# Two-layer hybrid decoder step: eight-step convolutions laid between matmul blocks, and S5 products held back by a count of recent instructions

## The chip, the cores and the metric

The kernel runs on one core of one Trainium2 chip. The metric is the device time of one execution in microseconds (us). The engines are named as the profile names them: PE (TensorE, with PEld for its weight loads), DVE (VectorE), ACT (ScalarE), POOL (GpSimd) and SP (SyncE, which here only issues DMAs).

## The reference

For 288 token columns (one prompt of 256 tokens and eight sequences of four new tokens) two layers are computed, each of a mixer, a feed-forward part and an embedding part. What the change touches is in the mixer:

```
z = x @ w_in                                   # 2048 -> u (1024), cv (1024), cg (1024)
y5, h = _s5(u, ...)                            # 64 groups: B u, complex scan over tokens, C h + D u
g5 = gelu(y5); s5_out = g5 * sigmoid(g5 @ s5_w_glu)
c = cv * sigmoid(cg)                           # GLU
c, new_conv = causal_dwconv(c, conv_buf, conv_w, conv_b)   # depthwise, 31 taps
c = silu(LN(c))
mix = concat(s5_out, c) @ w_out
```

The feed-forward part (2048 to 2 x 5632 and back, with a 3-tap convolution) and the embedding part follow, each with a LayerNorm. All is float32.

## The kernel before, in words

**Large products.** Weights come as blocks of 128 x 128, eight to a 512 KB load on SP (`stream_dma`, line 183). ACT makes a rounded half `whi`, DVE the rest `wlo`. `run` (line 354) works through a phase's list of blocks; each block is three matmuls of 288 columns into one accumulator (lines 379, 384, 385). At every second block `next_block` (line 217) calls `tick` (line 259), which emits what else is due.

**The planner.** The program is written out by a planner in Python, in a fixed order for every engine. It carries a clock `pe_t` for PE: 400 ns for a block, 500 for a convolution step, 400, 1000 and 1500 for the three kinds of S5 product. Deferred work (`defer`, `at`, generators that `wait`) is emitted when that clock, or a count of ticks, has come far enough.

**Phases of the mixer.** `u0` gives the first four u chunks. Then for j = 0..7 phase `p{j}` (32 blocks) gives the value and gate half of conv chunk j, and for j = 1..4 a phase `v{j}` (16 blocks) gives a further u chunk. Then comes `g` (64 blocks, the product with `s5_w_glu`, whose inputs are the S5 results), then `o`.

**A conv chunk.** When both halves of chunk j are there, ACT and DVE make the GLU into `cbuf` (one buffer, loaded with the cached rows by POOL at the start of loop j, line 1225), and POOL sends it to DRAM (`cb_d`, line 1246). `stack(j)` (line 1182) reads it back in four shifted copies (four DMAs on POOL, for j = 7 on SP) and sends the new cache rows out. `taps(j)` (line 1178) loads the tap weights `cw` (one buffer, 512 KB, POOL). `conv(j)` (line 1204) then makes the chunk in eight steps; each step is four matmuls of 32 weight columns and 256 token columns (line 1215) and four of 32 token columns (line 1218), each carried out in two passes, so 16 matmuls and 16 weight loads. Then ACT copies the result with the bias to `cvo`, and `ln_acc` takes it into the LayerNorm sums.

**Order around it.** At the end of phase `p{j}` the whole of `conv(j - 2)` stands, with a `tick` ahead of each step; then `taps(j - 1)`, the GLU if it was not yet emitted, and `stack(j)` (lines 1250 to 1256). `conv(6)` and `conv(7)` stand in the phase `g`: after 20 blocks of it `conv(6)` and `taps(7)`, after 12 more `conv(7)` (lines 1276 to 1281). While `conv(5)` is made, `split_g` splits S5 results for `g`, one per step from step 4 on. In the phase `g` itself, `xs_g` splits whatever is ready, at each block.

**S5.** The S5 runs as generators beside this, in eight chunks c. Each has small matmuls of 32 weight columns: `inject` (64 matmuls, line 1013), `project` (96, line 1042) and, in layer 0 and for layer 1 ahead of time, `s5_steps` (16, line 800), all through `strips` (line 395) or line 807. Between them stand a scan on DVE, elementwise work on ACT and POOL, and trips through DRAM on SP's and POOL's queues (`ust`, `tm`, `y_d`).

Of the kernel before, what the change touches and what calls it, by code (L numbers as in the profile page):

```python
# [16 lines left out]
SEQ = 256  # L17
# [47 lines left out]
L0_LAG = 4000.0  # L65
LOOK = 1
FREE_LAG = 500.0
EARLY_LAG = 7000.0
EARLY_RATE = 0.5
EV_GAP = 10  # L70
# [88 lines left out]
class Core:  # L159
    def __init__(self, tc, a, ctx):  # L160
        self.tc, self.nc, self.a, self.ctx = tc, tc.nc, a, ctx
        self.V = Meter(self, tc.nc.vector)
        self.pe_t = self.pe_l = self.dve_t = self.dve_c = 0.0
        self.freed = []
        self.scan = None
        self.rate = SETUP_RATE
        self.bg = []
        self.late, self.timed = [], []
        self.evq, self.ev_pos, self.acc_n = [], 0, 0
        self.lz, self.lz_n = None, 0  # L170
        self.pos = 0
        self.next_dma = 0
        self.next_hi = 0
        self.next_lo = 0
        self.raw = {}
        self.sub = {}
        self.nblk = DEPTH * NBLK
        self.early = {}


    def stream_dma(self, upto):
# [67 lines left out]
    def run_timed(self, force=False):  # L249
        for x in list(self.timed):  # L250
            if force or x[0] <= self.pe_t:
                self.timed.remove(x)
                x[1]()

    def flush(self):
        while self.late:
# [96 lines left out]
    def run(self, blocks, xs, evac, sums=None, wide=False):  # L353

        nc = self.nc
        tot, seen, accs = sums or self.sums(blocks)
        k0, pend = blocks[0][1], []
        for _, k, m in blocks:
            if pend and k != k0:
                for out, w, xl in pend:  # L360
                    nc.tensor.matmul(out, w, xl, start=False, stop=False)  # L361
                pend = []
            w = self.next_block()
            if m not in accs:
                if wide and len(accs) == 4:
                    accs[m] = (1 << 30, self.ps.tile([P, 512], F32, tag="one", name="acc5", bufs=1))
                else:
                    t = self.acc_tile()
                    accs[m] = (self.acc_n, t)
            out = accs[m][1][:, :TOK]  # L370
            n = seen[m]
            first, last = n == 0, n == tot[m] - 1
            if len(w) == 1:
                self.pe_t += 485.0
                nc.tensor.matmul(out, w[0], self.x32[k], start=first, stop=last)
            else:
                xh, xl = xs(k)
                self.pe_t += 400.0
                nc.tensor.matmul(out, w[0], xh, start=first, stop=False)  # L379
                if k == k0 and not last and (pend or not seen[m]):  # L380
                    nc.tensor.matmul(out, w[1], xh, start=False, stop=False)  # L381
                    pend.append((out, w[0], xl))
                else:
                    nc.tensor.matmul(out, w[0], xl, start=False, stop=False)  # L384
                    nc.tensor.matmul(out, w[1], xh, start=False, stop=last)  # L385
            seen[m] += 1
            if last:
                a, t = accs.pop(m)
                self.evq.append((a, lambda m=m, t=t: evac(m, t[:, :TOK])))
            if self.evq and self.pos - self.ev_pos >= EV_GAP:  # L390
                self.evict()
        while self.evq:
            self.evict()

# [405 lines left out]
    def s5_steps(self, bs, pw, kp):  # L800

        nc = self.nc
        kps = self.ps.tile([P, 512], F32, tag="one", name="kps", bufs=1)
        self.pe_t += 400.0
        for i in range(2):
            for q in range(4):
                nc.tensor.matmul(kps[32 * q:32 * q + 32, :4 * CIN], bs[:, q, i].rearrange("p g c -> p (g c)"),
                                 pw[:, q, i, 0:4].rearrange("p k o -> p (k o)"), start=(i == 0), stop=(i == 1),
                                 tile_position=(0, 32 * q))
        kv = kps[:, :4 * CIN].rearrange("p (k o) -> p k o", o=CIN)  # L810
        for g in range(2):
            nc.scalar.activation(kp[:, 3:7, g], kv, AF.Copy, scale=self.mask2[:, g:g + 1])
# [47 lines left out]
    def s5(self, l, mp):  # L860
# [88 lines left out]
        def make_o(c, cc, bc=None):  # L949

            if early:
                pk = cc
            else:
                yield from self.s5_out(l, c, cc, bc, pw, bs, work)
                yield from self.wait(PJ_LAG)
                while state["y"]:
                    yield None
                state["k"] = True
                self.s5_steps(bs, pw, kp)
                self.at(PS_LAG + 500.0, lambda: state.update(k=False))  # L960
                yield None
                k0 = kp[:, 3].rearrange("p g o -> p (g o)")
                V.scalar_tensor_tensor(k0, self.eye, self.prm("s5_d", c), k0, op0=OP.mult, op1=OP.add)
                kd = self.dp.tile([P, 7 * 2 * CIN], F32, tag="k_d", name="k_d", bufs=2)
                G.dma_start(kd, kp.rearrange("p k g o -> p (k g o)"))
                pk = pw[:, :, :, 1:5]
            while state["p"] < c - 1:
                yield None
            of = om.rearrange("p q i (r g o) -> p (q i) r g o", g=2, o=CIN)
            pf = pk.rearrange("p q i k o -> p (q i) k o")  # L970
            for g in range(2):
                h = slice(g * ST, (g + 1) * ST)
                nc.scalar.activation(of[h, :, :, g], pf[h], AF.Copy)
            if early:
                self.at(PS_LAG, lambda: state.update(o=c))
                return

            def back():
                load_t(c, kd)
                self.at(LOAD_LAG, lambda: state.update(o=c))  # L980
            self.at(BACK_LAG, back)
# [17 lines left out]
        def inject(us):  # L999
            v = self.ps.tile([P, 2, 512], F32, tag="two", name="bu", bufs=1)  # L1000
            self.pe_t += 1000.0
            for q in range(4):
                for i in range(2):
                    self.strips(v[:, i, q * NCH:(q + 1) * NCH], em[:, q, i], us[:, q], True, True)
# [37 lines left out]
        def project(c, us):  # L1042
            y = self.ps.tile([P, 512], F32, tag="one", name="y", bufs=1)
            self.pe_t += 1500.0
            for q in range(4):
                o = y[:, q * NCH:(q + 1) * NCH]
                self.strips(o, tms[c % 2][:, q], us[:, q], True, False)
# [56 lines left out]
        def main():  # L1104
# [3 lines left out]
            tb = tables(0)  # L1108
            initial()
            for c in range(S5C):  # L1110
                while c not in ready or state["e"] < c:
                    yield None
                self.rate = RATE[l]
                v = inject(us[c])
# [15 lines left out]
        def tail(c, us):  # L1130
            yield from self.wait(PJ_LAG)
            while finals:
                finals.pop(0)()
            while state["o"] < c or state["k"]:
                yield None
            state["y"] = True
            y = project(c, us)
# [21 lines left out]
    def mixer(self, l, ph):  # L1159
        nc, a = self.nc, self.a  # L1160
        V = self.V
        with self.tc.tile_pool(name="mx", bufs=1) as mp:
# [40 lines left out]
                    gsplit.add(c)  # L1203
                    n -= 1

            def conv(j):
                st, cw = stacks.pop(j), cws.pop(j)
                o = self.acc_tile()
                for k in range(8):
                    self.tick()  # L1210
                    self.pe_t += 500.0
                    if j == CVC - 3 and k >= 4:
                        split_g(n=1)
                    for b in range(4):
                        nc.tensor.matmul(o[32 * b:32 * b + 32, :SEQ], cw[:, b, k], st[:, b, 4 * k:4 * k + SEQ],  # L1215
                                         start=(k == 0), stop=False, tile_position=(0, 32 * b))
                    for b in range(4):
                        nc.tensor.matmul(o[32 * b:32 * b + 32, SEQ:TOK], cw[:, b, k], window(st, b, CW + 4 * k),
                                         start=False, stop=(k == 7), tile_position=(0, 32 * b))
                nc.scalar.activation(cvo[j], o[:, :TOK], AF.Identity, bias=self.prm("conv_b", j))  # L1220
                self.ln_acc(cst, cvo[j], j == CVC - 1)

            for j in range(CVC):
                cb = mp.tile([P, CBW], F32, tag="cbuf", name="cbuf", bufs=1)
# [2 lines left out]
                cbuf[j] = (cb, d)  # L1227
                part = {}

                def ev(m, acc):  # L1230
                    t = mp.tile([P, TOK], F32, tag="cvt", name="cvt", bufs=3)
                    if m < 16:
                        nc.scalar.activation(t, acc, AF.Copy, scale=0.5)
# [13 lines left out]
                        part["done"] = True  # L1247
                    self.defer(2, glu)
                self.run(ph[f"p{j}"], self.xs, ev)
                if j > 1:  # L1250
                    conv(j - 2)
                if j:
                    taps(j - 1)
                while "done" not in part:
                    self.late.pop(0)[1]()
                stack(j)
                if j in U_AT:
                    self.run(ph[f"v{j}"], self.xs, ev_u)

# [14 lines left out]
                self.split_x(m, w, 0.25)  # L1274
            sums = self.sums(ph["g"])
            self.run(ph["g"][:G_CUT[0] - 12], xs_g, ev_g, sums)
            conv(CVC - 2)
            taps(CVC - 1)
            self.run(ph["g"][G_CUT[0] - 12:G_CUT[0]], xs_g, ev_g, sums)
            self.finish(scan)  # L1280
            conv(CVC - 1)

            def fill(z):
                self.run(ph["g"][G_CUT[z]:G_CUT[z + 1]], xs_g, ev_g, sums)
# [347 lines left out]
```

## Time and profile before

| | |
|---|---|
| runs | 2738.88, 2741.99, 2744.91 us; median 2741.99 |
| the profiled execution's own time | 2743.43 us |
| its span, first to last instruction | 2741.6 us |
| mean granted clock | 0.991 |
| busy: PE / PEld / DVE / ACT / POOL | 97% / 95% / 66% / 49% / 11% |
| mixer of layer 0, about | 0 to 300 us |
| mixer of layer 1, about | 1378 to 1670 us |

The timeline's rows read: start, duration, engine, line, operation, output and inputs, sizes, count, and in brackets the idle time of the engine before it with what ended it ("issue": nothing that the profile shows). Matmuls overlap in the pipeline, so the pitch from start to start is their cost, not their duration. In a row of the windows, each engine's busy time stands with the number of its instructions, then the granted clock of PE (1.00 is full), the DMA engines' busy share and GB/s.

### The profile page before, as it was taken

Reading aid. Unit: us, or ns where it says so; the run is one execution under the profiler, and the core shown is the slowest. Engines: PE = TensorE matmul, PEld = TensorE weight load, DVE = VectorE, ACT = ScalarE, POOL = GpSimd, SP = SyncE. Lnnn points to the kernel's source line nnn. Section 1 sums busy time; section 2 is a strip of 40 time slices with the busy share of each in tenths; the row PEclk is TensorE's granted clock in tenths of the full one; section 3 lists DMA queues with packets and bytes.
Section 4 is the critical chain, followed back from the end, with each engine's and each line's share of the span. In section 5 each row is a group of like instructions: output and inputs, shape, how many; then the busy total and the mean of one; then the engine's idle time right before and its main releaser. Section 6 shows DMA issues by size and latency. Waiting matters only on the chain. (4 is left out here: it accounts for less than half of the span.)

```text
span 2741.6 us, 57943 instructions
## 1 busy us (share of the span) xinstructions
PE 2660.2 (97%) x23696; PEld 2600.8 (95%) x23696; DVE 1808.4 (66%) x3016; ACT 1352.9 (49%) x2224; POOL 305.0 (11%) x913
## 2 busy tenths in 40 slices
PE   8898999999999999999998899999999999999997
PEld 7887999999999999999987889999999999999997
DVE  6885768665677546667876558676546664566686
ACT  3453547553455345546464435565435553455363
POOL 3442001000011000000034410010000000000000
PEclk9999999999999999999999999999999999999998
DMA  7988444456566654554468775445554555455442
GB/s 236 254 249 248 151 153 162 162 192 190 186 190 197 201 167 159 174 172 153 164 191 257 229 204 180 154 159 171 175 169 157 169 174 171 156 169 176 164 151 102
DMA packets 188042, 496.12 MB, mean 181 GB/s; under 512 B 46369, under 2 KB 72241, under 8 KB 187521
## 3 DMA queue, kind: packets, MB, share of 16 engines
q1 hardware_dynamic: 174592, 444.00, 49.9%
q0 software_dynamic: 13184, 48.42, 6.2%
q8 instruction: 186, 3.05, 0.5%
q14 instruction: 80, 0.65, 0.1%
HBM read 472.11 MB, written 24.87 MB: 181 GB/s over the span
## 5 line engine op out<-in xcount | busy, mean ns | idle before, releaser
L379 PE MATMUL acc<-xh,whi 128*128 128x288 f32 x4656 | 1377.4, 296 | 8.1 <-ACT e L1333 3.2
L384 PE MATMUL acc<-xl,whi 128*128 128x288 f32 x4357 | 1288.0, 296 | 4.6 <-issue 3.7
L385 PE MATMUL acc<-xh,wlo 128*128 128x288 f32 x4357 | 1286.4, 295 | 0.0
L202 ACT ACTIVATE whi<-wraw 128x1024 fp32r<-128x1024 f32 x766 | 791.8, 1051 | 344.7 <-PE acc L384 206.1
L145 DVE TENSOR_TENSOR wlo<-wraw,whi 128x1024 fp32r<-128x1024 f32 x766 | 921.3, 1225 | 41.6 <-ACT whi L202 23.9
L379 PEld LDWEIGHTS acc<-xh,whi 128*128 128x128 f32 x4656 | 877.7, 189 | 15.8 <-ACT e L1333 4.1
L385 PEld LDWEIGHTS acc<-xh,wlo 128*128 128x128 f32 x4357 | 820.5, 188 | 3.9 <-issue 3.9
L384 PEld LDWEIGHTS acc<-xl,whi 128*128 128x128 f32 x4357 | 820.7, 188 | 3.0 <-DVE xl L145 2.5
L379 PE MATMUL acc<-hh,whi 128*128 128x288 f32 x1408 | 416.3, 296 | 0.0
L145 DVE SCALAR_TENSOR_TENSOR fo<-fe,parf,fo 128x304 f32<-128x304 f32 x352 | 188.2, 535 | 323.0 <-ACT fo L1366 316.6
L385 PE MATMUL acc<-hh,wlo 128*128 128x288 f32 x1312 | 387.7, 296 | 0.0
L384 PE MATMUL acc<-hl,whi 128*128 128x288 f32 x1312 | 386.9, 295 | 0.0
L379 PEld LDWEIGHTS acc<-hh,whi 128*128 128x128 f32 x1408 | 265.2, 188 | 0.5
L384 PEld LDWEIGHTS acc<-hl,whi 128*128 128x128 f32 x1312 | 247.0, 188 | 0.0
L385 PEld LDWEIGHTS acc<-hh,wlo 128*128 128x128 f32 x1312 | 246.6, 188 | 0.0
L1362 ACT ACTIVATE fe<-acc 128x256 f32<-128x256 f32 x176 | 67.4, 383 | 290.2 <-PE acc L385 290.2
L1372 POOL COPY fstage<-fe 128x9 f32<-128x9 f32 x176 | 44.5, 253 | 1038.1 <-ACT fe L1363 1016.7
L438 ACT ACTIVATE ln_q<-x 128x288 f32<-128x288 f32 x90 | 40.1, 446 | 221.1 <-DVE x L145 221.1
L1366 ACT ACTIVATE fo<-fe,parf 128x304 f32<-128x304 f32 x176 | 113.1, 642 | 16.7 <-ACT fe L1363 0.4
L145 DVE TENSOR_TENSOR x<-x,acc 128x288 f32<-128x288 f32 x64 | 29.1, 454 | 139.1 <-PE acc L385 139.0
L1386 ACT ACTIVATE hh<-fth 128x288 fp32r<-128x288 f32 x88 | 39.2, 445 | 163.5 <-DVE fth L145 163.5
L145 DVE SCALAR_TENSOR_TENSOR x<-x,acc 128x288 f32<-128x288 f32 x64 | 29.0, 453 | 122.9 <-PE acc L385 122.8
(251 smaller groups left out, 2340.7 us busy)
## 6 DMA issues: line engine op xcount, KB each, us to landing
wraw<-in_wts_dram SPq DMA_DIRECT2D x776, 512.0 KB
stack<-cb_d POOLq DMA_DIRECT2D x32, 282.0 KB, 9.3
cw<-in_convw_dram POOLq DMA_DIRECT2D x16, 512.0 KB, 5.3
big<-cb_d POOLq DMA_DIRECT2D x24, 282.0 KB, 9.6
cbuf<-in_convi_dram POOLq DMA_DIRECT2D x16, 283.5 KB, 9.6
cb_d<-cbuf POOLq DMA_DIRECT2D x16, 283.5 KB, 3.6
out_dram<-cb_d POOLq DMA_DIRECT2D x16, 283.5 KB, 11.5
sbt<-in_s5b_dram SPq DMA_DIRECT2D x15, 256.0 KB
```

Source lines behind the costliest of these rows:

```text
L145: return f(out, *args, **kw)
L202: self.nc.scalar.activation(hi, self.raw[s], AF.Copy)
L379: nc.tensor.matmul(out, w[0], xh, start=first, stop=False)
L384: nc.tensor.matmul(out, w[0], xl, start=False, stop=False)
L385: nc.tensor.matmul(out, w[1], xh, start=False, stop=last)
L438: nc.scalar.activation(st["q"], v, AF.Square)
L1362: nc.scalar.activation(e[:, 2:2 + SEQ], acc[:, :SEQ], AF.Copy)
L1366: nc.scalar.activation(o[:, :w], e[:, 2:EW], AF.Identity, bias=self.prm("ffn_conv_b", m), scale=self.prm("ffn_conv_w2", m))
L1372: nc.gpsimd.tensor_copy(stage[:, z, :, 0], e[:, SEQ:EW:6])
L1386: nc.scalar.activation(hh[i], h, AF.Copy, scale=0.5)
```

## The change

`conv(j)` no longer emits its steps; it gives back eight functions. For j = 0..5 they are put in `self.side`, and `run` emits one after each block of the phase that follows. `taps(j - 1)` and `stack(j)` are emitted after the last of them (`behind`), and the GLU of chunk j ahead of the first. `conv(6)` and `conv(7)` are emitted in one piece as before (`conv_now`, which first empties `side`). Besides, every small product notes a count of instructions with the planner's clock (32 for a conv step, 64, 128 and 192 for `s5_steps`, `inject` and `project`), and the three S5 products wait until those of the last 6000 ns and their own make at most 420.

```diff
+ISSUE_SPAN = 6000.0
+ISSUE_MAX = 420
...
+    def room(self, n):
+
+        self.issued = [x for x in self.issued if x[0] > self.pe_t - ISSUE_SPAN]
+        return sum(x[1] for x in self.issued) + n <= ISSUE_MAX
+
+    def spent(self, n):
+        self.issued.append((self.pe_t, n))
...
             if self.evq and self.pos - self.ev_pos >= EV_GAP:
                 self.evict()
+            if self.side:
+                self.side.pop(0)()
...
-                while state["y"]:
+                while state["y"] or not self.room(64):
...
-                while c not in ready or state["e"] < c:
+                while c not in ready or state["e"] < c or not self.room(128):
...
-            while state["o"] < c or state["k"]:
+            while state["o"] < c or state["k"] or not self.room(192):
...
-            def conv(j):
-                st, cw = stacks.pop(j), cws.pop(j)
-                o = self.acc_tile()
-                for k in range(8):
-                    self.tick()
+            def conv(j, behind=None):
+
+                st, cw, o = stacks.pop(j), cws.pop(j), []
+
+                def step(k):
+                    if not k:
+                        o.append(self.acc_tile())
                     self.pe_t += 500.0
+                    self.spent(32)
...
+                    if k == 7:
+                        nc.scalar.activation(cvo[j], o[0][:, :TOK], AF.Identity, bias=self.prm("conv_b", j))
+                        self.ln_acc(cst, cvo[j], j == CVC - 1)
+                        if behind:
+                            behind()
+                return [lambda k=k: step(k) for k in range(8)]
+
+            def conv_now(j):
+                while self.side:
+                    self.side.pop(0)()
+                for f in conv(j):
+                    self.tick()
+                    f()
...
                 self.run(ph[f"p{j}"], self.xs, ev)
-                if j > 1:
-                    conv(j - 2)
-                if j:
-                    taps(j - 1)
+
+                def behind(j=j):
+                    if j:
+                        taps(j - 1)
+                    stack(j)
                 while "done" not in part:
                     self.late.pop(0)[1]()
-                stack(j)
+                while self.side:
+                    self.side.pop(0)()
+                if j > 1:
+                    self.side = conv(j - 2, behind)
+                else:
+                    behind()
...
-            conv(CVC - 2)
+            conv_now(CVC - 2)
             taps(CVC - 1)
             self.run(ph["g"][G_CUT[0] - 12:G_CUT[0]], xs_g, ev_g, sums)
             self.finish(scan)
-            conv(CVC - 1)
+            conv_now(CVC - 1)
```

## Rows read from the trace of the kernel before

**Rows 1.** Windows: the two mixers and the stretch between (PE, PEld, DVE, ACT, POOL).

```profile
82.00:282.00 200.00, 180.21 (x3053) 160.41 (x3043) 143.56 (x252) 90.43 (x173) 72.92 (x136) 0.97 0.85 242
1392.00:1636.00 244.00, 223.09 (x3499) 205.69 (x3499) 145.05 (x213) 114.44 (x194) 85.29 (x154) 0.99 0.80 237
300.00:1360.00 1060.00, 1057.74 (x8069) 1053.57 (x8069) 719.48 (x1178) 540.53 (x881) 53.46 (x272) 1.00 0.53 175
```

**Rows 2.** Waits of PE (total us, times, longest us), five of the list.

```profile
PE y L399 <- issue: 4.3, 2, 2.8
PE acc L384 <- issue: 3.7, 1, 3.7
...
PE acc L1218 <- issue: 3.4, 3, 1.4
...
PE acc L379 <- issue: 2.2, 1, 2.2
...
PE acc L361 <- DVE xl L145: 1.5, 2, 1.0
```

**Rows 3.** Groups by line, PE: the conv matmuls of 256 columns, both buffers.

```profile
L1215 PE MATMUL acc<-big,cw 128*32 128x256 f32 x512 | 36.5, 401 | 5.8 <-issue 3.5 <-ACT xh L538 2.2
L1215 PE MATMUL acc<-stack,cw 128*32 128x256 f32 x512 | 33.9, 387 | 0.0
```

**Rows 4.** Timeline of PE, 107.9 to 113.3 us: one conv chunk and its neighbours.

```profile
108.28 0.29 PE L385 MATMUL acc<-xh,wlo 128*128 128x288 f32 x1
...
109.02 0.62 PE L1215 MATMUL acc<-stack,cw 128*32 128x256 f32 x8
...
111.99 0.62 PE L1215 MATMUL acc<-stack,cw 128*32 128x256 f32 x8
...
112.84 0.29 PE L381 MATMUL acc<-xh,wlo 128*128 128x288 f32 x1
112.97 0.29 PE L361 MATMUL acc<-xl,whi 128*128 128x288 f32 x1
```

**Rows 5.** Timeline of PE, 102.4 to 103.8 us: a lone product of 16 small matmuls.

```profile
102.71 0.29 PE L385 MATMUL acc<-xh,wlo 128*128 128x288 f32 x1
102.93 0.43 PE L807 MATMUL kps<-pw,bsm 128*32 128x64 f32 x16
...
103.53 0.29 PE L384 MATMUL acc<-xl,whi 128*128 128x288 f32 x1
```

**Rows 6.** The page, queues: the larger instruction queue (packets, MB, share).

```profile
q8 instruction: 186, 3.05, 0.5%
```

**Rows 7.** Windows, PE alone, from one "issue" wait's end to the next.

```profile
211.12:216.79 5.67, 4.16 (x126) 1.00 0.89 275
...
1461.66:1510.53 48.87, 44.97 (x886) 0.97 0.79 240
```

**Rows 8.** Timeline of PE: S5 products that waited in or just after a conv chunk.

```profile
151.32 0.33 PE L399 MATMUL y<-ust,tm 128*32 128x72 f32 x8 [1.55 <-ACT kp L812]
...
207.15 0.47 PE L399 MATMUL bu<-ust,em 128*32 128x72 f32 x17 [0.73 <-DMA ust<-u_d]
...
1504.70 0.41 PE L399 MATMUL bu<-ust,em 128*32 128x72 f32 x13 [1.14 <-ACT stb L996]
...
1539.71 0.47 PE L399 MATMUL bu<-ust,em 128*32 128x72 f32 x8 [3.57 <-DMA ust<-u_d]
```

**Rows 9.** The tile `cw`, 240 to 290 us: its two loads, issue to landing.

```profile
L1180 POOL DMA_DIRECT2D cw<-in_convw_dram x2: 538/548/557, 253.7 to 264.9; - x2
...
DMA to landing us min/median/max: 5.3/6.7/8.1
```

**Rows 10.** Timelines at the start of `g` in layer 0: PE, ACT, DVE.

```profile
246.60 0.29 PE L385 MATMUL acc<-xh,wlo 128*128 128x288 f32 x1
...
247.24 1.43 ACT L538 ACTIVATE xh<-u 128x288 fp32r<-128x288 f32 x4
...
252.31 0.53 DVE L145 SCALAR_TENSOR_TENSOR cbuf<-cvt 128x256 f32<-128x256 f32 x2 [9.11 <-DMA cbuf<-in_convi_dram]
```

More of the change, by code (lines that the diff above doesn't have):

```diff
@@ L178, in __init__ @@
         self.early = {}
+        self.side, self.issued = [], []
     def stream_dma(self, upto):
@@ L804, in s5_steps @@
         self.pe_t += 400.0
+        self.spent(64)
         for i in range(2):
@@ L1001, in inject @@
             self.pe_t += 1000.0
+            self.spent(128)
             for q in range(4):
@@ L1044, in project @@
             self.pe_t += 1500.0
+            self.spent(192)
             for q in range(4):
@@ L1214, in conv @@
                     for b in range(4):
-                        nc.tensor.matmul(o[32 * b:32 * b + 32, :SEQ], cw[:, b, k], st[:, b, 4 * k:4 * k + SEQ],
+                        nc.tensor.matmul(o[0][32 * b:32 * b + 32, :SEQ], cw[:, b, k], st[:, b, 4 * k:4 * k + SEQ],
                                          start=(k == 0), stop=False, tile_position=(0, 32 * b))
                     for b in range(4):
-                        nc.tensor.matmul(o[32 * b:32 * b + 32, SEQ:TOK], cw[:, b, k], window(st, b, CW + 4 * k),
+                        nc.tensor.matmul(o[0][32 * b:32 * b + 32, SEQ:TOK], cw[:, b, k],
+                                         window(st, b, CW + 4 * k),
                                          start=False, stop=(k == 7), tile_position=(0, 32 * b))
-                nc.scalar.activation(cvo[j], o[:, :TOK], AF.Identity, bias=self.prm("conv_b", j))
-                self.ln_acc(cst, cvo[j], j == CVC - 1)
+                    if k == 7:
[10 more added lines that the diff above has]
+                    f()
             for j in range(CVC):
@@ L1228, in mixer, with ev @@
                 part = {}
-                def ev(m, acc):
+                def ev(m, acc, cb=cb, d=d, part=part):
                     t = mp.tile([P, TOK], F32, tag="cvt", name="cvt", bufs=3)
```

## The prediction

> **What bounds the kernel now.** I read first the windows by stage. Between 300 and 1360 us PE is busy for 1057.7 of 1060 us: nothing that the change touches can help there. In the two mixers it is busy for 180.2 of 200 and 223.1 of 244 us, so 19.8 + 20.9 = 40.7 us are idle, while the DMA engines are at 0.85 and 0.80 against 0.53 elsewhere [rows 1]. So the mixer is bound by PE too, with waits worth 1.5% of the span strewn in.
>
> Then I read who ended those waits. "Issue" stands at 4.3 us (S5 products), 3.4 (inside conv chunks), 3.7 and 2.2 (plain blocks), seven waits and 13.6 us [rows 2]; the conv line shows another 3.5 [rows 3], but that one is the last chunk's and is `cw` landing late (below). The seven have a pattern. From the end of one to the next PE does 126 matmuls, or 886, which is 7 x 126.6 [rows 7]; with the weight loads 126 make 252 instructions, some 256 with the waits. The instruction queue moved 186 packets and 3.05 MB [rows 6], 16.4 KB each, 64 bytes for each of 256. So I take these waits for PE running out of instructions at the end of a packet. A packet lasts long in plain blocks (6 instructions in three pitches of 0.13 us, so 17 us) and 4.3 us in a conv chunk, whose 8 steps hold 256.
>
> The remaining idle time is S5 data arriving late and `cw`.
>
> **The change part by part.**
>
> *Laying the steps apart* adds PE time. In the chunk shown, the last block matmul starts at 108.28 and the second one behind the chunk at 112.84: 4.56 us, less two ordinary pitches of 0.13, leaves 4.30 for the chunk. Its middle steps come every (111.99 - 109.02) / 6 = 0.495 us [rows 4]. Eight make 3.96; the other 0.34 is what it costs to go from 128-column to 32-column matmuls and back, once. A lone product shows that this is paid by short groups as well: 16 small matmuls between blocks take 103.53 - 102.71 - 0.26 = 0.56 us [rows 5], with the same 0.22 us ahead of the first and 0.23 behind the first block matmul. A step alone between two blocks therefore costs 0.83 us, and eight of them 6.64 instead of 4.30. Chunks 0 to 5 are laid apart, in two layers: 12 x 7 x 0.336 = **+28.2 us**. The count of steps does not change (1024 matmuls of 256 columns, 16 chunks x 8 steps x 8 [rows 3]). This is all on PE, which is the bound, so I hide nothing of it here; what it covers is counted below.
>
> *"Issue" waits.* A laid step and its block are 38 instructions in 1.22 us, so a packet of them lasts 8.2 us instead of 4.3. That helps the 7.7 us that lie at products and in chunks. But a `project` is still 192 instructions in one piece, and with two steps behind it a packet is gone in under 4 us, less than the 5.67 us in which one packet was used up and still had to be waited for [rows 7]. The 3.7 and 2.2 us in plain blocks have no chunk near them. I take 70% of 7.7, **-5.4**; ends 0 and -13.6.
>
> *The count for S5 products* adds a wait in the planner. Laid steps come at 900 ns of its clock, at most seven in 6000 ns, 224; with `project` 416, under 420. So it holds something back only when two S5 products and several steps fall together. I price it at 0: a product moves by a few blocks, and what is queued behind it is its own chunk's scan. If it bit, S5 would reach `g` later; a late input there costs what the two shown cost, 1.5 together [rows 2].
>
> *S5 waits in or behind chunks.* Four, 1.55 + 0.73 + 1.14 + 3.57 = 7.0 us [rows 8]. They are waits for things set off at a given point of the planner's clock, and PE now takes longer per ns of it. Half, **-3.5**; ends 0 and -7.0.
>
> *DMAs that move with the step.* `taps(j - 1)`, the four loads of `stack(j)` and the store behind them now start after eight blocks of the next phase, 9.8 us (8 x 1.22) into it. On POOL they move behind the load of `cbuf(j + 1)` for j = 5 and 6. For chunks up to 5, 24 to 40 blocks remain, 9.5 us or more; the `cw` loads shown landed in 5.3 and 8.1 us [rows 9], so I take 0, and 2 at worst. On SP the loads of `stack(7)` wait for chunk 5 with weight units behind them; units are loaded three or four ahead, so 0. `cw` for `conv(6)` is another matter: before, 20 blocks lay between, now 12 (4.8 us). That is exactly the place of `conv(7)`, which waits 3.5 and 2.2 us for its `cw` today [rows 3]. I take 2 in each layer, **+4.0**; ends 0 and +5.7.
>
> *Start of `g`.* `conv(5)` covered the first split of S5's results. Now the first block waits for `xh`: 247.24 + 0.36 (a quarter of 1.43) - 246.73 = 0.9 us a layer. Against that DVE's 9.11 us wait for `cbuf(7)` [rows 10], which holds up the GLU and behind it `xl` (the 1.5 us [rows 2]), should go, because that load moves ahead of the stack loads on POOL. Net **+0.5**. Were the load no earlier, `xl` would come at 253.2 where PE needs it by about 249, so +4 a layer.
>
> Sum: 28.2 - 5.4 - 3.5 + 4.0 + 0.5 = **+23.8 us**. The profiled execution had a span of 2741.6 and took 2743.43, so it would take 2767.2. It lies 1.44 above the median of the runs, 2741.99; against that median I predict **2765.8**.
>
> **The rivals.**
>
> *The instruction waits stay.* Packets may be late whatever PE does, since it is the loaded DMA that delays them (0.89 in the shortest window [rows 7]). Then the sum is 28.2 - 3.5 + 4.0 + 0.5 = 29.2, 2771.2 us. For it: the two waits in plain blocks. Against: five of seven lie at bursts. [...]
>
> *Everything is covered.* All 13.6 and 7.0 us go and `cw` is in time: 28.2 - 20.6 + 0.5 = 8.1, 2750.1 us. It needs every `project` to escape.
>
> *PE is not the mixer's bound* (the other side). If S5's trips through DRAM and the loaded DMA engines set the pace, the added PE time fills idle time, and the evener stream ends the waits: at most 28.2 - 40.7 = -12.5, 2729.5 us. It decides as soon as more than 28.2 of the 40.7 us is waiting for S5 and instructions in the laid stretches. For it: the DMA share, DVE at 144 of 200 us [rows 1]. Against: 13.6 + 7.0 = 20.6 us is all I find there; most of the rest lies ahead of the first chunk or at `conv(7)`, where no step is laid.
>
> *Half of the change does nothing*: the count never bites. That is in my forecast already, at 0.
>
> **How the numbers follow.** About 0.2% (5.5 us) can be told from no change. My forecast has 0.67, its own range 2755 to 2778; the waits that stay 0.13; all covered 0.10, of which a quarter falls within 0.2%; the DMA-paced mixer 0.10, of which a third would end within 0.2%, no lower than 2736.5. That makes slower 0.875, same 0.055, faster 0.07. The worst ends, 28.2 + 0.5 + 5.7 + 2, give 2778.4; the best of the forecast, 8.1, gives 2750. The range 2748 to 2778 leaves out the DMA-paced case, some of the covered one and a late `cbuf(7)`.
>
> **What would show it.** In the changed kernel's timeline a step of 16 matmuls between two blocks, with 1.22 us from block to block. In the windows, PE busier in the mixers and both mixers longer by some 12 us. Among the waits, "issue" near 8 us, with `project` as its place; `cw` ahead of `conv(6)`; `xh` at the first block of `g`; DVE's wait for `cbuf` gone. I am wrong if a lone step costs near 0.5 us, if "issue" goes to nothing and S5's waits with it, or if PE's idle time in the mixers shrinks by more than 28 us.

## The result and the profile after

The changed kernel takes 2766.97 us (median of 6 runs, 2761.69 to 2771.72) against 2741.49 for the kernel before on the same chips: ratio 1.0094, interval 1.0082 to 1.0105. It is slower, by 25.5 us. Forecast were 2765.8 and +23.8.

Windows of the changed kernel, PE alone (busy, matmuls, granted clock, DMA share, GB/s), cut at the first `inject` and at the LayerNorm of the conv in each layer:

```profile
57.20:305.90 248.70, 226.37 (x3496) 0.96 0.79 226
305.90:1434.60 1128.70, 1119.58 (x8502) 1.00 0.54 174
1434.60:1675.70 241.10, 222.56 (x3374) 0.95 0.74 221
1675.70:2768.50 1092.80, 1071.16 (x8068) 0.99 0.50 162
```

The same cut of the kernel before:

```profile
58.60:294.90 236.30, 214.43 (x3497) 0.96 0.83 237
294.90:1423.60 1128.70, 1119.98 (x8503) 1.00 0.53 174
1423.60:1648.90 225.30, 204.69 (x3374) 0.98 0.80 237
1648.90:2741.60 1092.70, 1071.14 (x8068) 0.99 0.49 162
```

Outside the mixers nothing moved by more than 0.1 us, apart from 1.4 us ahead of the first window. The mixers are 12.4 and 15.8 us longer, for the same matmuls, and PE is busier by 11.9 and 17.9. The step between two blocks, in the timeline of the changed kernel; to be held against [rows 4]:

```profile
111.97 0.64 PE L1234 MATMUL acc<-stack,cw 128*32 128x256 f32 x8
112.43 0.24 PE L1237 MATMUL acc<-stack,cw 128*32 128x32 f32 x8
112.60 0.40 PE L390 MATMUL acc<-xh,whi 128*128 128x288 f32 x1
112.84 0.29 PE L395 MATMUL acc<-xl,whi 128*128 128x288 f32 x1
112.97 0.29 PE L396 MATMUL acc<-xh,wlo 128*128 128x288 f32 x1
113.19 0.64 PE L1234 MATMUL acc<-stack,cw 128*32 128x256 f32 x8
```

From step to step 1.22 us, as worked out. The waits of PE in the changed kernel, which answer to [rows 2]:

```profile
PE bu L412 <- ACT em L961: 12.5, 8, 6.6
...
PE acc L390 <- ACT xh L551: 6.6, 2, 4.8
PE bu L412 <- DMA ust<-u_d: 5.7, 2, 5.5
...
PE acc L392 <- DVE wlo L147: 5.2, 1, 5.2
PE acc L1234 <- issue: 4.1, 2, 2.2
PE acc L395 <- issue: 3.3, 1, 3.3
...
PE acc L390 <- issue: 0.6, 1, 0.6
```

Two lines of the kernel before, to hold `ust` and `em` against:

```profile
PE bu L399 <- DMA ust<-u_d: 7.8, 4, 3.6
...
PE bu L399 <- ACT em L947: 6.5, 8, 4.0
```

The last two lines of the changed kernel are all that is left of the waits for instructions: 3.9 us of 13.6. The 4.1 us on the conv line are `conv(6)` waiting for its taps, in both layers (in layer 1 the load landed at 1644.90 us, and the first matmul started at 1644.99). But `em`, `xh` and `wlo` have grown or are new. I sum the idle time of PE over 0.1 us in both mixers: 43.0 before, 41.0 after.

What changed, in us, from the two traces:

| term | forecast | in the traces |
|---|---|---|
| trips between 128-column and 32-column matmuls (47 before, 129 after, counted; 0.336 each) | +28.2 | +27.6 |
| waits for instructions | -5.4 | -9.7 (13.6 to 3.9) |
| taps at `conv(6)` and `conv(7)` | +4.0 | -1.6 (5.7 to 4.1) |
| start of `g` (`xl` before, `xh` after) | +0.5 | +5.1 (1.5 to 6.6) |
| S5's waits, all | -3.5 | -1.1 (22.2 to 21.1) |
| `wlo` | 0 | +5.2 |
| rest of the mixers, what is left over | 0 | +2.7 |
| ahead of the first window | 0 | -1.4 |
| sum | +23.8 | +26.8; the spans differ by 26.9 |

The first row is a count times the price of the prediction. The rows of waits come from one execution of each kernel, and they move by themselves: the two price kernels below have the mixers of the kernel before, instruction for instruction, and in their traces PE is idle there for 41.5 and 33.9 us, with 11.8 and 9.6 us of waits for instructions, 2.8 and 3.1 for the taps of `conv(7)`, and 11.0 and 7.4 for `em`. So these rows hold to some us only.

### The profile page after: what moved, and what is told of

The parts are those of the page before. It is cut to its first block, busy times and chain, and to the rows that moved or that the text cites. A ratio compares the mean times of both kernels' runs of the same rounds, so it can differ in the third digit from the quotient of the medians.

```text
span 2768.5 us, 57948 instructions
## 1 busy us (share of the span) xinstructions
PE 2690.5 (97%) x23696; PEld 2612.1 (94%) x23696; DVE 1806.2 (65%) x3016; ACT 1352.5 (49%) x2224; POOL 307.7 (11%) x913
## 4 chain that ended last, share of the span: by engine, by line
PE 85%; DMA 6%; DVE 3%; issue 2%; ACT 1%; POOL 1%; SPq 1%; ACTq 0%; DVEq 0%; POOLq 0%
PE acc L390 27%; PE acc L395 25%; PE acc L396 25%; DMA wraw<-in_wts_dram 2%; PE acc L1234 2%; PE acc L372 2%; PE acc L392 2%; DMA y_d<-yw 1%; DVE wlo L147 1%; DMA cbuf<-in_convi_dram 1%; DMA k_d<-kp 1%; DVE x L147 1%; DVE ln_n L147 0%; PE y L412 0%; PE lnp L482 0%
## 5 line engine op out<-in xcount | busy, mean ns | idle before, releaser
L390 PE MATMUL acc<-xh,whi 128*128 128x288 f32 x4656 | 1386.3, 298 | 13.1 <-ACT xh L551 6.6
L390 PEld LDWEIGHTS acc<-xh,whi 128*128 128x128 f32 x4656 | 878.3, 189 | 23.8 <-ACT xh L551 7.1
## 6 DMA issues: line engine op xcount, KB each, us to landing
out_dram<-cb_d POOLq DMA_DIRECT2D x16, 283.5 KB, 11.2
```

## The experiments

Ratios are to the kernel before, in runs of the same job.

**The price of a lone step by itself.** Into the kernel before go 96 steps with unused results, in the second down-projection of each layer, where PE is never idle (busy for 160.00 of 160.00 us from 1000 to 1160): as `dummy(1)` each (the 16 matmuls of one step), or in pieces of eight, with `% 16` and `dummy(8)`.

```diff
+            if self.extra > 0:
+                self.extra_n += 1
+                if self.extra_n % 2 == 0:
+                    self.extra -= 1
+                    self.dummy(1)
```

> The kernel before with 96 conv-like steps more (16 small matmuls each, result unused), one after every second block of the second down-projection, where PE never waits: the price of a lone step by itself. My theory: 0.83 us each, 79.7 us more, 2818 us. Rival (a lone step costs what one in a chunk costs, 0.54 us): 51.6 us more, 2790 us.

> The same 96 steps in 12 pieces of eight, one piece after every 16th block of the same phases. My theory: 12 x 4.30 = 51.6 us more, 2790 us, so 28 us under the lone ones. Rival: the same as the lone ones within 4 us.

2821.20 and 2793.07 us; ratios 1.0287 (1.0264 to 1.0310) and 1.0194 (1.0169 to 1.0218): 82.4 and 54.3 us more, where 79.7 and 51.6 were forecast. The stretch from the conv LayerNorm to layer 1's first `inject` holds half of the steps and no mixer. Timelines of PE, first with lone steps, then with pieces of eight:

```profile
295.10 0.41 PE L535 MATMUL acc<-ln_q,ones_d 96*128 96x288 f32 x1
...
1463.43 0.40 PE L414 MATMUL bu<-ust,em 128*32 128x72 f32 x12
```

```profile
288.51 0.41 PE L535 MATMUL acc<-ln_q,ones_d 96*128 96x288 f32 x1
...
1442.96 0.33 PE L414 MATMUL bu<-ust,em 128*32 128x72 f32 x8
```

The stretch is 1168.33 and 1154.45 us long, against 1128.7 without. So 48 lone steps cost 39.6, **0.825 us each**, and six pieces 25.7, **4.29 each**. For 96 steps that is 27.8 us apart, and the times are 28.1 apart: the first term of the sum is shown, away from all S5 and all waits.

**Which half of the change it is.** The count for S5 products alone (`room`, `spent` and the three waits, put into the kernel before), and the changed kernel without the limit, by this edit:

```diff
-ISSUE_MAX = 420
+ISSUE_MAX = 1 << 30
```

> The kernel before with the count for S5 products alone; conv chunks in one piece. My theory (each lone conv step costs 0.34 us more than one in a chunk, and that is the loss): no change beyond the waits, ratio 0.995 to 1.002, PE waits put down to issue between 5 and 13.6 us, since a chunk of 256 now keeps products out for a while. Rival (holding back the S5 products starves the end of S5 and is the loss): slower, 2750 to 2770 us.

> The changed kernel without the count: steps laid between the blocks, S5 products never held back. My theory: as the changed kernel, 2762 to 2772 us, issue waits 3 to 7 us. Rival (the count is what loses or wins something of its own): off by more than 6 us from the changed kernel.

2736.04 us, ratio 0.9990 (0.9977 to 1.0004), and 2770.74 us, ratio 1.0119 (1.0100 to 1.0138). Both are as forecast, with 6.7 and 5.7 us of waits for instructions. All of the loss is the laying. The count costs nothing; with a limit of 420 its gain is too small to tell, alone and with the steps laid (1.0119 without it and 1.0094 with it, in runs of two jobs, and the intervals touch).

**Fewer trips.** `run` emits two steps after every second block, as in the edit, or eight after every eighth; the loads that follow a chunk stay where the change put them.

```diff
             if self.side:
-                self.side.pop(0)()
+                self.side_n += 1
+                if self.side_n % 2 == 0:
+                    for _ in range(2):
+                        self.side.pop(0)()
```

> The changed kernel with two steps after every second block, so four trips a chunk in place of eight; all DMAs that follow a chunk stay where the change put them. My theory: 12 x 4 x 0.336 = 16 us less than the changed kernel, 2748 to 2754 us. Rival (what loses is the later start of the tap and stack loads and of the split for g, or waits for weights): as the changed kernel, 2763 to 2770 us.

> The changed kernel with all eight steps in one piece after the eighth block of the next phase: one trip a chunk, the moved order and the count kept. My theory: 28 us of trips less, some 4 to 8 us of issue waits more: 2741 to 2749 us. Rival (the moved order is the loss): 2760 us or more.

2755.45 us, 1.0062 (1.0046 to 1.0078), and 2756.36 us, 1.0073 (1.0053 to 1.0093). The first is clearly under the changed kernel, but 1.5 us over its range: 48 trips less, 16 us by my price, gave 11.5 us between the medians and 8.8 by the ratios. The second missed mine by 7 us at the least. It has 51 trips, as few as I meant it to have, but PE is idle for 54.4 us in the mixers of the profiled execution, which was the longest of its six (2766.72 us). Its waits:

```profile
PE bu L416 <- ACT em L965: 19.6, 13, 5.9
...
PE y L416 <- DMA tm<-k_d: 7.9, 2, 4.0
```

In it the planner emits a whole chunk without a `tick`, so S5 stands still for a chunk. The next run puts the ticks back:

```diff
+                    for _ in range(8):
+                        self.tick()
+                        self.side.pop(0)()
```

> The changed kernel with each chunk in one piece after the eighth block, as in the run with eight together, but with the planner's tick ahead of each step as in the kernel before, so that S5 goes on inside the chunk. If the extra waits of that run came from S5 standing still for a chunk: 2739 to 2747 us, idle before PE in the mixers 35 to 45 us. Rival (the later tap and stack loads make the waits): 2752 to 2760 us, idle 50 us or more.

2747.96 us, 1.0028 (1.0016 to 1.0041), 1 us over the range, idle 39.7 us, 50 trips. Most of that run's excess was S5 standing still, but not all: against the count alone (0.9990, idle 31.7 us, 50 trips) there remain 10 us, though chunk and trips are the same. What differs is that chunk, GLU order, taps and stack loads stand eight blocks later. PE's waits of the late chunk:

```profile
PE bu L417 <- ACT em L966: 13.4, 9, 5.2
...
PE acc L391 <- ACT xh L556: 3.6, 2, 1.8
...
PE acc L393 <- DVE wlo L147: 2.5, 1, 2.5
```

These are the same three names as in the changed kernel. So the later order is a cost of its own, some 10 us, which my sum had as waits with both signs and about nothing in all. The changed kernel, too, emits its laid steps without the `tick` that stood ahead of each; what that costs there was not tried.

**What holds up `em`, `xh` and `wlo`.** The timeline of ACT around the longest wait of the changed kernel:

```profile
165.34 1.06 ACT L205 ACTIVATE whi<-wraw 128x1024 fp32r<-128x1024 f32 x1 [7.82 <-DMA wraw<-in_wts_dram]
166.31 1.32 ACT L961 ACTIVATE em<-sw,mask 128x512 f32<-128x512 f32 x2
```

The wait of SP's queue just before it, and then SP's timeline:

```profile
SPq L769 <- DMA sqb<-q_d: 4.8, 1, 4.8
```

```profile
162.97 0.33 SPq L189 DMA_DIRECT2D wraw<-in_wts_dram  x1
```

The unit of weights was issued only at 162.97, after SP had stood 4.8 us at a small S5 load. ACT, in order, stood 7.82 us at the copy of that unit, with `em` behind it, for which PE waited. The place belongs to the laid steps, the chain to this execution: this `inject`, the sixth of layer 0, waited 4.2 to 6.6 us in the four other kernels of this document that lay steps one or two at a time too, but there for `ust`; in the nine with chunks in one piece it waited 1.4 us at most. At the start of `g` ACT of the changed kernel stands at a weight copy again:

```profile
256.21 1.06 ACT L205 ACTIVATE whi<-wraw 128x1024 fp32r<-128x1024 f32 x1 [2.93 <-DMA wraw<-in_wts_dram]
257.17 2.42 ACT L551 ACTIVATE xh<-u 128x288 fp32r<-128x288 f32 x7
```

Here SP had not stood at an S5 load: its longest wait between 240 and 262 us, 5.5 us, is for a weight buffer that DVE's `wlo` frees. One line takes the split out from behind the copy:

```diff
+            split_g()
             sums = self.sums(ph["g"])
```

> The changed kernel with one line more: the S5 results that are ready are split for g ahead of the first block of g, so that on ACT the split stands ahead of the weight copy which that block's unit brings. My theory (the wait for xh at the start of g, 4.8 and 1.8 us, is ACT standing in order behind a weight copy whose load is late): about 1 us in each layer is left, 3 to 5 us less, 2761 to 2765 us. Rival (the split itself is what takes the time): xh waits as before and 2764 to 2770 us.

The split now stands ahead of the copy, and the waits of that run show what is left of `xh`:

```profile
PE acc L390 <- ACT xh L551: 1.7, 2, 0.8
```

6.6 became 1.7, so the cause of this wait is shown. The time, 2765.02 us, 1.0091 (1.0077 to 1.0104), can't be told from the changed kernel's.

`wlo` is late for another reason. The timeline of POOL, and then the waits of all engines from 1515 to 1523 us, in the changed kernel:

```profile
1499.45 0.58 POOL L1196 DMA_DIRECT2D cw<-in_convw_dram  x1
1500.03 2.21 POOL L1204 DMA_DIRECT2D stack<-cb_d  x4
1502.24 0.52 POOL L1206 DMA_DIRECT2D out_dram<-cb_d  x1
...
1505.21 0.54 POOL L1081 DMA_DIRECT2D y_d<-yw  x1
```

```profile
DVE yw L147 <- ACT yw L1074: 9.7, 1, 9.7
ACT yw L1071 <- DMA y_d<-yw: 6.7, 1, 6.7
...
PE acc L392 <- DVE wlo L147: 5.2, 1, 5.2
```

S5's store `y_d` was issued behind the tap and stack loads that the change moved there, and landed 12.9 us later. ACT stood for it, DVE for ACT, and `wlo` behind that on DVE. In all five kernels with laid steps this store took 12.1 to 13.1 us to land, and PE waited 4.9 to 5.3 us for `wlo`; in the seven with chunks in their old place it took 3.7 to 5.9 us, and `wlo` cost at most 1.1. The order is read from the rows; no run puts these loads back alone.

**Chunk 5 as before.**

```diff
-                if j > 1:
+                if j == CVC - 1:
+                    for f in conv(j - 2, behind):
+                        self.tick()
+                        f()
+                elif j > 1:
                     self.side = conv(j - 2, behind)
```

> The changed kernel with chunk 5 in one piece ahead of g, as before the change; chunks 0 to 4 laid apart. My theory: 14 trips less (4.7 us), no wait for xh at the start of g (6.6), no wait for the taps at conv(6) (4.1), and the last chunk waits again (up to 5.7): 2754 to 2760 us. Rival (g is not where the moved order costs): 2761 us or more.

2751.28 us, 1.0044 (1.0029 to 1.0060), 2.7 us better than the best of my range: the last chunk waited 0.5 us where I had up to 5.7. A sixth of the laying, the one at `g`, makes about half of the loss: 14 trips (4.7 us), and waits.

**Are these waits for instructions?** The kernel before with 128 PE instructions more near 29 us:

```diff
-        for s in range(4):
+        for s in (0, 1, 2, 3) * 3:
```

> The kernel before with the first layer's 16 transposes of the S5 tables made three times, 128 PE instructions more near 29 us and nothing else: half a packet. If the issue waits are PE at the end of a packet of 256 instructions: they stand elsewhere in the program, half a packet on, the counts of matmuls between them are still whole multiples of 126 to 127, and their sum may be anything from 5 to 20 us. Rival (they belong to certain products): the same places, the same sum.

2743.02 us in its one run. Windows of PE from one such wait's end to the next:

```profile
129.16:144.49 15.33, 14.63 (x254) 1.00 0.84 248
144.49:226.23 81.74, 72.59 (x1265) 0.96 0.86 229
226.23:234.05 7.82, 6.74 (x127) 1.00 0.90 270
234.05:239.20 5.15, 3.60 (x128) 1.00 0.72 170
1499.80:1515.36 15.56, 14.83 (x252) 1.00 0.90 267
```

254, 1265, 127, 128 and 252 matmuls are 2, 10, 1, 1 and 2 times 126 to 128, which with as many weight loads are 252 to 256 instructions. The waits stand at other places: the two in plain blocks, 2.17 and 3.74 us before, are gone, though no block, step or product has moved. All such waits of this trace sum to 8.0 us, within my range. So it is the end of a packet of 256 that decides, not the kind of matmul.

**A version that beats both.** The count alone, the last tap load earlier, then, in the second of the two kernels only, the limit lowered:

```diff
-            self.run(ph["g"][:G_CUT[0] - 12], xs_g, ev_g, sums)
+            self.run(ph["g"][:G_CUT[0] - 18], xs_g, ev_g, sums)
...
-            self.run(ph["g"][G_CUT[0] - 12:G_CUT[0]], xs_g, ev_g, sums)
+            self.run(ph["g"][G_CUT[0] - 18:G_CUT[0]], xs_g, ev_g, sums)
...
-ISSUE_MAX = 420
+ISSUE_MAX = 300
```

> The kernel with the count alone, and conv(6) with the last tap load after 14 blocks of g in place of 20, so that 18 blocks stand between that load and the last chunk. My theory (the last chunk waits for a load that lands 7 to 8 us after its issue, 4.8 us of blocks covering it): the waits of 3.5 and 2.2 us at the last chunk fall to about 1 and 0, 3 to 5 us under the kernel with the count alone. Rival (conv(6) now waits for its own taps instead): no change.

> The kernel with the count alone and the last chunk's load earlier, with a limit of 300 in place of 420, so that no project follows an inject or a chunk within 6000 ns of the planner's clock. If the count is what lowers the issue waits: 2 to 6 us of them left and 2728 to 2734 us. Rival (products held back only move the waits, and S5 comes later): 2735 to 2742 us.

2735.96 us, 0.9987 (0.9974 to 1.0000): no gain over the count alone, whose profile had no wait at the last chunk left to win. With 300 it is **2726.87 us, 0.9949 (0.9936 to 0.9962)**, faster than both kernels, and 1 us under my range. Its waits of PE:

```profile
PE bu L410 <- ACT em L959: 10.5, 13, 5.0
...
PE acc L1233 <- issue: 4.3, 5, 1.5
...
PE acc L390 <- issue: 1.7, 1, 1.7
PE acc L1230 <- issue: 1.3, 3, 0.9
```

Of these 7.8 us put down to "issue" 1.1 are `conv(6)` and its taps, and the other 6.8 are waits for instructions, more than the 2 to 6 that I forecast and no less than with a limit of 420 (6.7 with the count alone, 11.2 with the tap load moved too). PE's idle time in the mixers is 28.0 us, against 31.7 and 37.1 with 420, and `ust`, 8.1 and 7.1 us there, is gone. So the gain in time is shown, but not that it comes from the supply of instructions.

## Why the prediction was right, step by step

*Laying the steps apart* was the term that decided, and it held: 28.2 forecast, 27.6 by the trips counted, 27.8 in the kernels that do nothing else. It came from one chunk and one lone product [rows 4, 5].

*"Issue" waits* went the way that I forecast, by more: I took 70% of 7.7 us, 5.4, and 9.7 went. With the 9.6 us of a price kernel for the same mixers it would be 5.7, so how far I was off is open. That laying lowers them is shown: they sum to 3.5 to 5.7 us in the five kernels with laid steps, and to 6.7 to 13.5 in the nine with chunks in one piece. But the reasons were bad: no `project` waits for instructions in the changed kernel, where I had put what is left, and the 2.17 us in plain blocks went, which I had left out for having no chunk near. The shifted kernel shows why: 128 PE instructions more took both waits in plain blocks away, 2.17 and 3.74 us, so a wait belongs to a place in the program's packets, and with a changed order other instructions stand there. The rival that they stay, 2771 us, is refuted by the same runs. In the kernel before seven of 186 packets were waited for, and in the shifted kernel two waits stand one packet of 256 apart, 5.15 us.

*S5 waits.* The four that I halved are gone, but others came, 6.8 us at the `inject` above and 4.7 at the fourth of layer 1, so that all together lost 1.1 us where I had 3.5.

*DMAs that move with the step.* Here a step failed: I asked whether the moved loads are in time for their own chunk, took 0, and did not ask what stands behind them in POOL's queue. S5's store does, and `wlo` cost 5.2 us. The late chunk has the same moved loads, and its 10 us are the order's price in all.

*Start of `g`*: 0.9 us a layer for `xh` is what the split costs (0.8 in the run that splits first), but 4.8 and 1.8 were paid, because the split stood on ACT behind a weight copy whose load was late. That `cbuf(7)` would no longer hold DVE came true: the wait for `xl` there is gone.

*Taps*: `conv(6)` waits, 4.1 us in all, as forecast (4.0), and 3.5 to 3.9 in the other kernels with chunk 5 laid. That `conv(7)` would stop waiting, 5.7 us, I had not seen.

*The count* was priced at 0, and costs nothing.

So the errors in the waits, -4.3, -5.6, +4.6, +2.4 and +5.2, with 1.3 for what is left over and the stretch ahead of the first window, nearly cancel, and the sum is 3.0 us off. The total was right by the first term; the rest was luck within a range that allowed for it. The rival on the other side, PE not being the mixer's bound, is refuted: PE's idle time in the mixers shrank by 2.0 us, not by 28.

## What to carry to other kernels

Before small matmuls are strewn among large ones, take the price of going to the other shape and back from a place where it happens once, and multiply by the number of places: here 0.34 us, 82 times. Keeping the lumps of small instructions apart from each other came cheaper here than taking them apart: the limit of 300 gained 0.4% with the lumps left whole, though by which wait is open. Loads that are moved meet other work in their queue (here a store of S5, which took 12.9 us to land behind them, and 3.7 to 5.9 with the chunks in their old place); ask what stands behind them, not only whether they are in time themselves. And a job that stood behind a weight copy on ACT waited for that copy's load, 7.82 and 2.93 us here; look what stands ahead of it before costing it by its own duration.

## What the runs showed of the hardware

By the page of the kernel before, matmuls and weight loads of PE are 254.8 to each of the 186 packets of the instruction queue [rows 6]:

```profile
PE 2660.2 (97%) x23696; PEld 2600.8 (95%) x23696; DVE 1808.4 (66%) x3016; ACT 1352.9 (49%) x2224; POOL 305.0 (11%) x913
```

In the trace of the kernel before each of the seven waits stands at 191 or 192 plus a whole multiple of 256 PE instructions (matmuls, weight loads and semaphore waits), and ends 1.2 to 1.7 us after a packet's landing; in the shifted kernel the windows above show the same spacing. During a wait of 6.63 us in the changed kernel, which ended at 167.06, the granted clock fell from 1.00 to 0.50 at about 164.0, and it rose again at 170.8. Windows of PE in the changed kernel:

```profile
160.00:165.00 5.00, 0.43 (x4) 0.90 0.99 292
165.00:170.00 5.00, 2.77 (x65) 0.50 0.88 281
170.00:175.00 5.00, 5.00 (x36) 0.92 0.93 285
```

Block matmuls started 0.24 us apart just before it rose and 0.13 us after, so the work behind this wait took longer too; that the wait is what lowered the clock no run shows. In the mixers PE was busy at 0.50 for 32.4 us, against 21.2 before, which may be the 2.7 us left over in the table.
